# Four small moves at the seams of a two-layer hybrid encoder: a modulation sum's bank, two splits, the last unit's weave, the decays' sums

## The chip, the cores and the metric

The kernel runs on one core of one Trainium2 chip. The metric is the device time of that core in microseconds (us), taken as the median of several runs. Engines are named as in the profile: PE multiplies matrices and writes to banks of the accumulation memory, PEld is its load of weights, DVE, ACT and POOL work element by element, and SP issues transfers (DMA). Each engine takes its own instructions in the order in which they were written, and waits on semaphores of the others.

## The reference, cut to what matters

The program is one forward pass of two layers on a sequence of 1024 tokens with 1024 channels. Layer 0 is an attention layer, layer 1 a state-space layer (SSD, run in both directions).

```
cond = silu(c)
for i in range(2):
    mod = cond @ mod_w[i] + mod_b[i]            # 3072 numbers: shift, scale, gate
    shift, scale, gate = split(mod, 3)
    hn = rms_norm(x, norm_w[i]) * (1 + scale) + shift
    if i == 0:  y = dilated_attention(hn)       # q, k, v, z = split(hn @ w_in); ... (o * silu(z)) @ w_out
    else:       y = bi_ssd(hn)                  # projections, convolution, decays from dt, scan; ... @ w_out
    x = x + gate * y
return rms_norm(x, final_norm_w)
```

In layer 0 there are 24 heads in three patterns of dilation, and the three outputs of a head position are weighted by a softmax over the patterns (`alpha`). In layer 1 `dt = softplus(dt_raw + bias)`, and the decays are exponentials of cumulative sums of `-dt * a` inside chunks of 128 tokens.

## The kernel before, in words

Activations lie channels by tokens, in tiles of 128 channels by 1024 tokens. A float32 product is made of three matmuls: each operand is split into a rounded high part (a cast on ACT, line 271) and the rest (a subtraction on DVE, line 272), and high by high, high by low and low by high are summed in one bank (`mm3`, lines 376 to 378; `out_items`, lines 1000 to 1002). So before a product can start, its weights and its input must have been split. The 27 tiles of the pool `big` hold inputs in split form, outputs of units and weights of the modulation.

The engines' instructions stand in the order in which Python calls them. A block of work is a list of items with a cost and a function, and `weave(main, side)` calls the side's items between the main's, spread in proportion to the costs.

**Layer 0** has twelve units, a unit being two heads of one pattern. For each unit `attn_dense` makes four blocks of products (q, k, v, z), each of 8 steps of 6 matmuls, and into these 32 steps the attention of the unit before is woven (`attn_items`): high and low parts of q and k (`high` on ACT, `low` on DVE, lines 648 to 657), `vprep` (transposes of v, line 633), and for eight blocks of tokens `A` (scores: four matmuls into a bank of the tag `a0`, of which there are two; masked maximum on DVE, line 690; exponential on ACT, line 695), `B` (transposes of the weights, line 704, into the one bank of the tag `a2`; copied out by DVE, line 706) and `C` (product with v, line 719, bank `a3`; multiplied on DVE into the unit's `act` tile, line 730). `stats` sends the maxima and sums out through `a2` (line 743). `vprep` writes to `a2` too.

The modulation of the later uses is computed during layer 0: for each block of 128 outputs DVE multiplies and adds (lines 182 to 188), and after every fourth block `mod_sum` sums over partitions on PE (line 212, four sums, each printed by the profile as two matmuls) into the bank `a2`, from which DVE reads (line 214, and line 217 for scales). There are eight such sums, between 151 and 513 us.

**The last unit has no next unit.** Its attention (11 in count from 0) is woven into `out0`, the output projection: `out_passes` makes four passes (two halves of the tokens, two halves of the outputs) of 12 steps, each of 12 matmuls. In the first pass the steps use the `act` tiles of the units 0 to 11 in order. `prep(r, k)` splits `act[k]` for the half r, and `get` splits up to three steps ahead; the tiles 9 to 11 are ready only after the last mixing over the patterns (`mix_items(3)`: statistics loaded, exponentials, ratios, a broadcast through memory, three products on DVE at line 804). So `first` runs nine steps of the first pass with the last attention in between, nine steps of the second pass with the mixing in between, and then the rest of both.

**Layer 1** begins with three blocks whose steps run alone, then group 0 of eight. Into the steps of group 0 `dt_items` is woven, which computes `dt` and the decays: `tok` and a series on DVE, `end` (`da`, line 1263), `rows` (cumulative sums of `da` on PE, line 1273, total at line 1281, copied by ACT and sent to memory), `back` (transposes of the sums, line 1295, then DVE). Empty items (`wait`) with a cost set the places. DVE also takes the convolution's taps there (line 1330).

Of the kernel before, what the change touches and what calls it, by code (L numbers as in the profile page):

```python
# [12 lines left out]
F32R = mybir.dt.float32r  # L13
# [4 lines left out]
P = 128  # L18
# [3 lines left out]
H2 = 512  # L22
# [33 lines left out]
def weave(main, side):  # L56

    tm = sum(it[0] for it in main) or 1
    tsd = sum(it[0] for it in side) or 1
    i = a = 0  # L60
    b = 0.0
    for c, f, *_ in main:
        f()
        a += c
        while i < len(side) and (b + side[i][0] / 2) / tsd <= a / tm:
            side[i][1]()
            b += side[i][0]
            i += 1
    while i < len(side):
        side[i][1]()  # L70
        i += 1
# [20 lines left out]
class Trunk:  # L92
# [114 lines left out]
    def mod_sum(self, i, b, accs):  # L207

        nc = self.nc
        p = self.bank("a2", [P, 4, P])  # L210
        for k in range(4):
            nc.tensor.matmul(p[:, k, :1], accs[:, k], self.ones[:, :1], start=True, stop=True)
        m = self.modv[i]
        nc.vector.tensor_add(m[:, b:b + 4], p[:, :, 0], self.vec[:, 16 + 24 * i + b:20 + 24 * i + b])
        if b < 16:
            d = b // 2
            nc.vector.scalar_tensor_tensor(self.gs[i][:, d:d + 2], m[:, b + 1:b + 4:2], 1.0,
                                           self.vec[:, 64 + 8 * i + d:66 + 8 * i + d], op0=OP.add, op1=OP.mult)
# [594 lines left out]
    def layer0(self):  # L813
# [80 lines left out]
        r, v = [[self.u(t, [P, H2], F32, n) for _ in range(2)] for t, n in (("pt", 4), ("sm", SM))]  # L894
        u = self.big()
# [60 lines left out]
        side = []  # L956
        mods = self.mod_items(0, list(range(16, 24))) + self.mod_items(1, list(range(24)))
        for u in range(12):
            weave(self.attn_dense(u), side)
            side = self.attn_items(u)  # L960
            k = -(-len(mods) // (7 - u)) if u < 7 else 0
            for i in range(k):
                side.insert(len(side) * (i + 1) // (k + 1), mods.pop(0))
            if UNITS[u][1] == 0 and u:
                m = self.mix_items(UNITS[u][0] - 1)
                n = len(side)
                for i, (at, f) in enumerate(m):
                    side.insert(round(at * n) + i, (1, f))
# [152 lines left out]
    def norm_items(self, st, t, n, item):  # L1121
# [10 lines left out]

        return [(1, total), (1, start), (1, end)] + [(1, lambda kt=kt: item(kt, st["r", t])) for kt in range(KT)]

    def out0(self, tail):


        nc, io = self.nc, self.io
        self.x1d = self.scratch("x1d", [KT, P, S])
        self.hn = hn = [[None] * KT for _ in range(2)]  # L1140
        xin, x1, cut, st = {}, {}, {}, [{} for _ in range(2)]

        def prep(r, k):
            if (r, k) not in cut:
                h = cut[r, k] = self.big(F32R)
                self.split(h[:, :H2], h[:, H2:], self.act[k][:, H2 * r:H2 * r + H2])

        def get(r):
            def f(kt):
                new = (r, kt) not in cut  # L1150
                for k in range(kt, min(kt + 3, 12)):
                    if r or k < 9 or kt >= 9:
                        prep(r, k)
                if new:
                    self.flush()
                return cut[r, kt]
            return f

        def ahead(kt):
            if 8 <= kt < 11:  # L1160
                prep(1, kt - 8)

        def load(r, m):
            xin[m] = self.u("xin", [P, H2], F32, 5)
            nc.sync.dma_start(xin[m], io["xT"][m][:, H2 * r:H2 * r + H2])

        def evac(r, m, t, n, a):
            if t == 0:
                x1[r, m] = self.u("x1", [P, H2], F32, 9)
            x = x1[r, m][:, t:t + n]  # L1170
            nc.vector.scalar_tensor_tensor(x, a, self.gate(0, m), xin[m][:, t:t + n], op0=OP.mult, op1=OP.add)
            nc.gpsimd.dma_start(self.x1d[m][:, H2 * r + t:H2 * r + t + n], x)
            self.sum_squares(st[r], m, x, t, n)

        def after(r, t, n):
            return self.norm_items(st[r], t, n, lambda kt, rstd: self.hn_tile(
                1, kt, H2 * r + t, n, x1[r, kt][:, t:t + n], rstd, hn))

        def first(ps):
            weave(ps[0][:9], tail[1][:1] + tail[0])  # L1180
            weave(ps[1][:9], tail[1][1:])
            self.phase("w1")
            nc.scalar.preload_act_table_set(LN_EXP)
            return [p[9:] for p in ps]

        return self.out_passes("wout0", 12, 4, get, ahead, load, evac, after, first)


# [28 lines left out]
    def dt_items(self):  # L1217
# [73 lines left out]
        def back():  # L1291
            self.lo_engine = nc.vector
            p = self.bank("a0", [P, C, 64], 2)
            for c in range(C):
# [9 lines left out]
        wait = (lambda: None)  # L1304
        return ([(200, wait), (100, tok), (100, ratio), (500, wait)]
                + [(80, lambda k=k: series(k)) for k in range(15, 1, -2)]
                + [(100, end), (300, wait), (100, rows), (200, wait), (100, back), (700, wait)])

    def group_dense(self, g):

# [380 lines left out]

    def main(self):
        self.setup()
        side = self.layer0()
        side = self.out0(side)
        side = self.layer1(side)
        self.out1(side)
        self.phase(None)
# [92 lines left out]
```

## Time and profile before

| what | value |
|---|---|
| runs | 1871.14 us median of 3 (1870.12 to 1874.98) |
| the profiled execution: own time | 1870.17 us |
| its span | 1868.0 us |
| PE busy | 1781.9 us (95%) |
| PEld busy | 1457.3 us (78%) |
| DVE busy | 1421.3 us (76%) |
| ACT busy | 956.5 us (51%) |
| POOL busy | 327.2 us (18%) |
| mean granted clock of PE | 0.982 of full |

A row of a timeline gives the start and the duration in us, the engine, the line, the operation with the tiles written and read, and in brackets the idle time of the engine just before and what ended it. A row of a table by stretches gives the stretch, its length, the busy time of each engine with the number of its instructions, the granted clock of PE, the busy share of the DMA engines and GB/s. Times are counted from the start of the span.

### The profile page before, as it was taken

Reading aid. Unit: us, or ns where it says so; the run is one execution under the profiler, and the core shown is the slowest. Engines: PE = TensorE matmul, PEld = TensorE weight load, DVE = VectorE, ACT = ScalarE, POOL = GpSimd, SP = SyncE. Lnnn points to the kernel's source line nnn. Section 1 sums busy time; section 2 is a strip of 40 time slices with the busy share of each in tenths; the row PEclk is TensorE's granted clock in tenths of the full one; section 3 lists DMA queues with packets and bytes.
Section 4 is the critical chain, followed back from the end, with each engine's and each line's share of the span. In section 5 each row is a group of like instructions: output and inputs, shape, how many; then the busy total and the mean of one; then the engine's idle time right before and its main releaser. Section 6 shows DMA issues by size and latency. Waiting matters only on the chain.

```text
span 1868.0 us, 28492 instructions
## 1 busy us (share of the span) xinstructions
PE 1781.9 (95%) x10050; PEld 1457.3 (78%) x10050; DVE 1421.3 (76%) x3219; ACT 956.5 (51%) x2095; POOL 327.2 (18%) x493
## 2 busy tenths in 40 slices
PE   5899999999999999999999999999999999789997
PEld 3678788778788888778978788888888878567787
DVE  7866578666755555666686989898998989897975
ACT  5454445444545544544435656565656565565632
POOL 4611112112211221010110101010101010224310
PEclk7899999999999999999999999999999999999998
DMA  6242234223411221264213233424334243344543
GB/s 252 92 124 89 84 107 132 66 89 91 125 47 55 58 77 52 68 213 139 96 51 84 75 111 75 117 82 115 89 93 105 76 111 82 113 123 143 187 158 101
DMA packets 99734, 193.66 MB, mean 104 GB/s; under 512 B 15624, under 2 KB 23048, under 8 KB 99592
## 3 DMA queue, kind: packets, MB, share of 16 engines
q1 hardware_dynamic: 86600, 167.32, 29.6%
q0 software_dynamic: 12288, 23.86, 4.7%
q8 instruction: 80, 1.31, 0.3%
q10 hardware_dynamic: 704, 0.66, 0.1%
q14 instruction: 62, 0.51, 0.1%
HBM read 169.00 MB, written 16.48 MB: 99 GB/s over the span
## 4 chain that ended last, share of the span: by engine, by line
PE 39%; DVE 11%; ACT 3%; DMA 2%; issue 2%; SPq 0%; POOL 0%; DVEq 0%; ACTq 0%; POOLq 0%
PE acc L376 8%; PE acc L378 7%; PE acc L377 7%; PE a L1481 3%; PE a L1419 2%; DVE big L1330 2%; PE a L1000 2%; PE a L1001 2%; PE a L1002 2%; DVE wlo L272 2%; PE acc L1002 1%; PE acc L1000 1%; PE acc L1001 1%; DVE W L1465 1%; DVE acs L1470 1%
## 5 line engine op out<-in xcount | busy, mean ns | idle before, releaser
L376 PE MATMUL acc<-big,whi 128*128 128x512 f32 (+1 forms) x1520 | 631.5, 415 | 12.6 <-ACT big L293 11.9
L377 PE MATMUL acc<-big,whi 128*128 128x512 f32 (+1 forms) x1520 | 595.7, 392 | 2.7 <-DVE big L294 2.6
L378 PE MATMUL acc<-big,wlo 128*128 128x512 f32 (+1 forms) x1520 | 596.4, 392 | 0.3 <-DVE wlo L272 0.3
L376 PEld LDWEIGHTS acc<-big,whi 128*128 128x128 f32 x1520 | 288.3, 190 | 78.3 <-issue 15.7
L378 PEld LDWEIGHTS acc<-big,wlo 128*128 128x128 f32 x1520 | 287.7, 189 | 64.4 <-DVE wlo L272 1.2
L377 PEld LDWEIGHTS acc<-big,whi 128*128 128x128 f32 x1520 | 288.9, 190 | 52.8 <-DVE big L294 5.9
L272 DVE TENSOR_TENSOR wlo<-wraw,whi 128x512 fp32r<-128x512 f32 (+1 forms) x297 | 215.4, 730 | 83.4 <-ACT whi L271 80.4
L271 ACT CAST whi<-wraw 128x512 fp32r<-128x512 f32 (+1 forms) x302 | 181.5, 612 | 82.8 <-PE a L1001 30.0
L695 ACT ACTIVATE sm<-sm,nb 128x256 f32<-128x256 f32 (+1 forms) x192 | 89.3, 466 | 198.8 <-DVE nb L693 196.1
L1330 DVE SCALAR_TENSOR_TENSOR big<-acc,cv,big 128x512 f32<-128x512 f32 (+1 forms) x248 | 169.4, 743 | 6.5 <-ACT big L1322 6.5
L1489 POOL TENSOR_TENSOR big<-big,yt 128x128 f32<-128x128 f32 x128 | 65.3, 530 | 588.2 <-DVE yt L1485 588.1
L1451 ACT ACTIVATE E<-E,nacb 128x128 f32<-128x128 f32 x256 | 81.9, 391 | 144.1 <-DVE E L1443 130.3
L706 DVE COPY pt<-a 128x512 f32<-128x512 f32 (+1 forms) x96 | 57.6, 600 | 76.6 <-PE a L704 76.5
L690 DVE CUSTOM_DVE_ANT_0 sm<-a,cst 128x256 f32<-128x256 f32 (+1 forms) x192 | 65.0, 376 | 65.1 <-PE a L685 64.8
L1000 PE MATMUL a<-big,whi 128*128 128x256 f32 (+1 forms) x304 | 99.3, 327 | 0.0
L1002 PE MATMUL a<-big,wlo 128*128 128x256 f32 (+1 forms) x304 | 98.2, 323 | 0.5 <-DVE wlo L272 0.5
L1001 PE MATMUL a<-big,whi 128*128 128x256 f32 (+1 forms) x304 | 97.9, 322 | 0.0
L1001 PE MATMUL acc<-big,whi 128*128 128x512 f32 x224 | 88.8, 396 | 6.1 <-DVE big L1556 4.3
L592 POOL DMA_DIRECT2D rt<-kT x92 | 50.3, 559 | 251.0 <-ACT kT L532 150.6
L1002 PE MATMUL acc<-big,wlo 128*128 128x512 f32 x224 | 89.3, 399 | 3.3 <-DVE wlo L272 2.7
L1000 PE MATMUL acc<-big,whi 128*128 128x512 f32 x224 | 90.5, 404 | 1.3 <-ACT big L271 1.2
L1322 ACT ACTIVATE big<-acc,cv 128x512 f32<-128x512 f32 x62 | 44.5, 769 | 86.4 <-PE acc L378 76.1
(254 smaller groups left out, 3186.6 us busy)
## 6 DMA issues: line engine op xcount, KB each, us to landing
wraw<-in_win SPq DMA_DIRECT2D x186, 256.0 KB
acs<-acsd SPq DMA_DIRECT2D x64, 512.0 KB
wraw<-in_wout SPq DMA_DIRECT2D x112, 256.0 KB
big<-in_modw SPq DMA_DIRECT2D x48, 512.0 KB
yd<-big POOLq DMA_DIRECT2D x14, 512.0 KB, 4.5
big<-yd SPq DMA_DIRECT2D x28, 256.0 KB
vT<-mix POOLq DMA_DIRECT2D x20, 256.0 KB, 4.7
big<-in_xT SPq DMA_DIRECT2D x8, 512.0 KB
```

Of the source, the lines that this page charges most:

```text
L271: self.nc.scalar.copy(dst_hi, src)
L272: self.late.append((lambda: self.lo_engine.tensor_sub(dst_lo, src, dst_hi.bitcast(F32)), tile))
L376: mm(o, hi[:, cols], x_[:, t0:t0 + n], start=first, stop=False, **kw)
L377: mm(o, hi[:, cols], x_[:, H2 + t0:H2 + t0 + n], start=False, stop=False, **kw)
L378: mm(o, lo[:, cols], x_[:, t0:t0 + n], start=False, stop=last, **kw)
L695: nc.scalar.activation(sm[:, h, :W], sm[:, h, :W], AF.Exp, bias=nb[:, h:h + 1], scale=0.125, accum_out=stat[:, h, 1, i:i + 1])
L1000: mm(o, hi[:, c], x[:, t:t + n], start=kt == 0 and (n == H2 or m % 2 == 0), stop=False, **kw)
L1001: mm(o, hi[:, c], x[:, H2 + t:H2 + t + n], start=False, stop=False, **kw)
L1002: mm(o, lo[:, c], x[:, t:t + n], start=False, stop=kt == nkt - 1, **kw)
L1330: nc.vector.scalar_tensor_tensor(y[:, lo:hi], a[:, lo + o:hi + o], w[:, cv, k:k + 1], y[:, lo:hi], op0=OP.mult, op1=OP.add)
L1451: nc.scalar.activation(E[:, h], E[:, h], AF.Exp, bias=self.nacb[:, c, 4 * g + h:4 * g + h + 1])
L1489: nc.gpsimd.tensor_mul(z, z, t[:, r])
```

## The change

It has four parts, and no operation is added or taken out.

1. `mod_sum` takes a bank of the tag `a0` (two, shared with the scores) in place of the one bank `a2`.
2. The splits of `act[0]` and `act[1]` for the first half of the tokens, made so far at the first step of the output projection, are called before the last of the 32 steps of unit 11. `prep` becomes the method `act_split` and its table the attribute `cut0`.
3. The last unit's attention is woven into 8 steps of the first pass instead of 9, and the mixing into the ninth step and the nine of the second pass.
4. In `dt_items` the empty item before `rows` costs 450 for 300, the one between `rows` and `back` 100 for 200, and the one after it 650 for 700: the sum stays 1200.

```diff
@@ def mod_sum(self, i, b, accs):
-        p = self.bank("a2", [P, 4, P])
+        p = self.bank("a0", [P, 4, P], 2)
@@ def layer0(self):
         for u in range(12):
-            weave(self.attn_dense(u), side)
+            d = self.attn_dense(u)
+            if u == 11:
+                for k in range(2):
+                    d.insert(len(d) - 1, (1, lambda k=k: self.act_split(0, k)))
+            weave(d, side)
@@
+    def act_split(self, r, k):
+
+        if (r, k) not in self.cut0:
+            h = self.cut0[r, k] = self.big(F32R)
+            self.split(h[:, :H2], h[:, H2:], self.act[k][:, H2 * r:H2 * r + H2])
+
     def out0(self, tail):
...
-        xin, x1, cut, st = {}, {}, {}, [{} for _ in range(2)]
-
-        def prep(r, k):
-            if (r, k) not in cut:
-                h = cut[r, k] = self.big(F32R)
-                self.split(h[:, :H2], h[:, H2:], self.act[k][:, H2 * r:H2 * r + H2])
+        xin, x1, cut, st = {}, {}, self.cut0, [{} for _ in range(2)]
+        prep = self.act_split
...
         def first(ps):
-            weave(ps[0][:9], tail[1][:1] + tail[0])
-            weave(ps[1][:9], tail[1][1:])
+            weave(ps[0][:8], tail[1][:1] + tail[0])
+            weave(ps[0][8:9] + ps[1][:9], tail[1][1:])
@@ def dt_items(self):
-                + [(100, end), (300, wait), (100, rows), (200, wait), (100, back), (700, wait)])
+                + [(100, end), (450, wait), (100, rows), (100, wait), (100, back), (650, wait)])
@@ def main(self):
         self.setup()
+        self.cut0 = {}
```

Three places show what this does to the order. The first is PE in unit 5's time, at the modulation sum that stands before unit 4's first transposes of v (L212 the sum into a bank, L633 the transposes into the bank `a2`; in brackets the semaphores waited for). Before:

```order
L378 MATMUL acc_3178<-big_612,wlo_3122 128x512
L212 MATMUL a_576_3276<-ones_67,big_2699 128x1 [waits DMAHW2_49,Activation_49]
L212 MATMUL a_576_3276<-ones_67,big_2699 128x1 x2
L212 MATMUL a_576_3276<-ones_67,big_2699 128x1 [waits DVE_49]
L633 MATMUL a_577_3283<-cst_71,vT_3010 128x128 [waits DVE_49]
L633 MATMUL a_577_3283<-cst_71,vT_3010 128x128 x3
```

Now:

```order
L378 MATMUL acc_3178<-big_612,wlo_3122 128x512
L212 MATMUL a_576_3276<-ones_67,big_2699 128x1 [waits DMAHW2_49]
L212 MATMUL a_576_3276<-ones_67,big_2699 128x1 x2
L212 MATMUL a_576_3276<-ones_67,big_2699 128x1 [waits DVE_49]
L633 MATMUL a_577_3283<-cst_71,vT_3010 128x128 [waits Activation_49]
L633 MATMUL a_577_3283<-cst_71,vT_3010 128x128 x3
```

No row moves; the transposes wait for ACT's copy out of `a2` instead of DVE's read of the sum.

The second is DVE from the end of unit 11's dense blocks into the output projection (L272 is the low part of a split: of an `act` tile where it writes `big`, of a weight where it writes `wlo`; L654 to L657 are the low parts of q and k, eight operations a half). Before, first the stretch with the first half of q and k, then the next rows:

```order
L272 TENSOR_TENSOR big_7062<-big_806,big_7062 128x512 [waits Activation_49]
L272 TENSOR_TENSOR big_7064<-big_1388,big_7064 128x512 [waits Activation_49]
L272 TENSOR_TENSOR big_7066<-big_1972,big_7066 128x512 [waits Activation_49]
L654 TENSOR_TENSOR Q_1252_7051<-kT_6631,Q_1252_7051 64x512 [waits DMASW5_49,DMASW1_49,Activation_49]
...
L272 TENSOR_TENSOR wlo_7075<-wraw_6874,whi_7074 128x512 [waits DMAHW3_49]
L272 TENSOR_TENSOR big_7107<-big_2524,big_7107 128x512 [waits Activation_49]
L272 TENSOR_TENSOR wlo_7113<-wraw_6952,whi_7112 128x512 [waits DMAHW4_49,PE_49,Activation_49]
L654 TENSOR_TENSOR Q_1252_7051<-kT_6631,Q_1252_7051 64x512 [waits Activation_49]
```

Now:

```order
L272 TENSOR_TENSOR big_7036<-big_806,big_7036 128x512 [waits Activation_49]
L272 TENSOR_TENSOR big_7038<-big_1388,big_7038 128x512 [waits Activation_49]
L654 TENSOR_TENSOR Q_1254_7057<-kT_6631,Q_1254_7057 64x512 [waits DMASW5_49,DMASW1_49,Activation_49]
...
L272 TENSOR_TENSOR big_7068<-big_1972,big_7068 128x512
L272 TENSOR_TENSOR wlo_7074<-wraw_6874,whi_7073 128x512 [waits DMAHW3_49]
L654 TENSOR_TENSOR Q_1254_7057<-kT_6631,Q_1254_7057 64x512 [waits Activation_49]
...
L272 TENSOR_TENSOR big_7107<-big_2524,big_7107 128x512
L272 TENSOR_TENSOR wlo_7113<-wraw_6952,whi_7112 128x512 [waits DMAHW4_49,PE_49,Activation_49]
```

The low part of `act[2]` now stands behind the first half of q and k, and that of `act[3]` with its weights behind the second half.

The third is PE in group 0 of layer 1, around `rows` (L1273 before, L1279 now; L1281 and L1287 its total). Before:

```order
L378 MATMUL acc_9146<-big_8716,wlo_9079 128x512
L1273 MATMUL a_1662_9184<-cst_71,big_9012 32x128 [waits DVE_49,PE_49]
L1273 MATMUL a_1662_9184<-cst_71,big_9012 32x128 x7
L1273 MATMUL a_1663_9194<-cst_71,big_9012 32x128 [waits PE_49]
L1273 MATMUL a_1663_9194<-cst_71,big_9012 32x128 x7
L1281 MATMUL a_1664_9205<-big_9012,ones_67 128x512 [waits Activation_49]
L376 MATMUL acc_9145<-big_8092,whi_9113 128x512
```

Now:

```order
L378 MATMUL acc_9146<-big_8716,wlo_9079 128x512
L376 MATMUL acc_9145<-big_8092,whi_9113 128x512 [waits Activation_49]
L377 MATMUL acc_9145<-big_8092,whi_9113 128x512
L378 MATMUL acc_9145<-big_8092,wlo_9114 128x512 [waits Pool_49]
L376 MATMUL acc_9146<-big_8721,whi_9113 128x512
L377 MATMUL acc_9146<-big_8721,whi_9113 128x512
L378 MATMUL acc_9146<-big_8721,wlo_9114 128x512
L1279 MATMUL a_1662_9192<-cst_71,big_9012 32x128 [waits DVE_49,PE_49]
L1279 MATMUL a_1662_9192<-cst_71,big_9012 32x128 x7
```

One step of six matmuls has moved ahead of `rows`; `back` stays where it was among the steps.

## Rows read from the trace of the kernel before

**Rows 1.** The page, part 1: busy time, share of the span, instructions.

```profile
PE 1781.9 (95%) x10050; PEld 1457.3 (78%) x10050; DVE 1421.3 (76%) x3219; ACT 956.5 (51%) x2095; POOL 327.2 (18%) x493
```

**Rows 2.** PE's waits, whole span: for whom; us in total, times, longest.

```profile
PE a L633 <- DVE modv L214: 4.0, 2, 3.7
...
PE a L704 <- DVE modv L214: 0.3, 1, 0.3
```

**Rows 3.** Timeline, 344 to 356 us: the fifth modulation sum.

```profile
349.51 0.69 DVE L654 TENSOR_TENSOR Q<-kT,Q 64x512 fp32r<-64x512 f32 x1
350.14 0.95 PE L212 MATMUL a<-ones,big 128*128 128x1 f32 x8
...
353.94 0.69 DVE L272 TENSOR_TENSOR wlo<-wraw,whi 128x512 fp32r<-128x512 f32 x1
354.54 0.15 DVE L214 TENSOR_TENSOR modv<-a,vec 128x4 f32<-128x4 f32 x1
...
354.76 1.11 PE L633 MATMUL a<-cst,vT 128*128 128x128 f32 x4 [3.67 <-DVE modv L214]
```

**Rows 4.** Busy time by stretches: us, PE, PEld, DVE, ACT, POOL, clock, DMA, GB/s.

```profile
124.00:128.00 4.00, 4.00 (x15) 3.28 (x14) 3.14 (x13) 2.22 (x9) 0.00 (x0) 0.59 0.68 227
...
354.76:360.00 5.24, 5.24 (x17) 4.46 (x18) 0.81 (x4) 3.82 (x4) 0.00 (x0) 0.50 0.46 150
...
967.20:971.80 4.60, 4.60 (x35) 3.48 (x36) 4.60 (x8) 1.16 (x2) 0.59 (x1) 0.63 0.02 4
...
1060.00:1085.00 25.00, 22.41 (x152) 17.71 (x151) 21.19 (x48) 19.35 (x39) 4.72 (x10) 1.00 0.28 94
```

**Rows 5.** Busy time by stretches, one stretch of dense steps alone.

```profile
940.00:950.00 10.00, 10.00 (x45) 8.26 (x45) 9.23 (x12) 3.66 (x7) 1.95 (x2) 1.00 0.12 32
```

**Rows 6.** Timeline, PE and DVE: the longest wait of scores, and the fourth sum.

```profile
123.43 0.39 PE L684 MATMUL a<-K,Q 128*128 128x256 f32 x1 [2.09 <-DVE stat L690]
...
297.95 0.08 DVE L690 DVE_READ_ACCUMULATOR2_ANT stat<- 128x1 f32 x1
298.06 0.94 PE L212 MATMUL a<-ones,big 128*128 128x1 f32 x8
```

**Rows 7.** Timeline, 748 to 765 us: from the last dense block into the output projection.

```profile
748.12 1.29 ACT L549 ACTIVATE big<-acc 128x512 f32<-128x512 f32 x2 [7.99 <-PE acc L378]
...
749.45 1.65 ACT L271 CAST big<-big 128x512 fp32r<-128x512 f32 x3
...
750.12 0.50 PE L1000 MATMUL acc<-big,whi 128*128 128x512 f32 x1 [1.23 <-ACT big L271]
...
757.20 0.69 DVE L272 TENSOR_TENSOR wlo<-wraw,whi 128x512 fp32r<-128x512 f32 x1
...
757.95 0.50 PE L1002 MATMUL acc<-big,wlo 128*128 128x512 f32 x1 [0.68 <-DVE wlo L272]
...
764.83 0.28 PE L685 MATMUL a<-L,Q 128*128 128x256 f32 x1
```

**Rows 8.** Timeline, PE, 783 to 816 us: last attention, statistics, ninth unit's tile.

```profile
783.57 0.41 PE L704 MATMUL a<-cst,sm 128*128 128x128 f32 x2 [1.31 <-DVE pt L706]
...
788.58 0.28 PE L743 MATMUL a<-cst,stat 128*32 128x128 f32 x1
...
815.07 0.50 PE L1001 MATMUL acc<-big,whi 128*128 128x512 f32 x1 [1.49 <-DVE big L272]
```

**Rows 9.** Timeline, 966 to 990 us: the decays' sums in layer 1.

```profile
967.20 3.10 PE L1273 MATMUL a<-cst,big 128*32 128x128 f32 x32 [3.10 <-DVE big L1263]
...
975.88 0.71 PE L1295 MATMUL a<-cst,big 64*128 64x64 f32 x8
...
984.40 1.07 ACT L1334 ACTIVATE big<-big 128x1024 f32<-128x1024 f32 x1
...
987.54 0.81 PE L1406 MATMUL a<-cst,big 128*128 128x128 f32 x6
```

**Rows 10.** Timeline, PE, layer 1's scan: a wait under 2 us.

```profile
1067.28 0.66 PE L1481 MATMUL a<-acs,SS 128*64 128x128 f32 x8 [1.94 <-DVE acs L1470]
```

## The prediction

> **What bounds the kernel now.** I read the page's table of engines first, then PE's waits, then the timeline at each of the four seams that the change touches, and last the table by stretches for the clock. PE is busy for 1781.9 of 1868.0 us [rows 1], so the kernel is faster only where PE stands still or runs at the half clock. Its waits at these seams are few and short. A modulation sum holds the transposes behind it three times: 3.67 us once, 0.33 once, and 0.3 before a transpose of weights [rows 2, 3]. At the first step of the output projection it waits 1.23 us for a split, and 0.68 at the third [rows 7]. The last attention has one wait of 1.31 between two neighbouring transposes, and the tile that needs the last mixing is 1.49 late [rows 8]. The decays' sums wait 3.10 [rows 9].
>
> The clock comes on top. Where PE stood 3.67 us, the next 5.24 us ran at a granted clock of 0.50, which is 1.2 GHz of the two levels [rows 3, 4]; after 3.10 us the next 4.60 ran at 0.63 in the mean [rows 4, 9]; after a wait of 2.09 four us ran at 0.59 [rows 4, 6]. After one of 1.94 the clock stayed at 1.00 [rows 4, 10].
>
> One dense matmul costs 10.00 us by 45, 0.222 us [rows 5]. So a step of layer 0 or 1 (6 matmuls) costs 1.33 us, one of the projection (12) 2.67 us.
>
> **Part 1, the sum's bank.** At 350 us the transposes (L633) wanted the one bank in which the sum lay, and DVE read that sum only after the eight operations of a half of q and k, from 349.51 to 353.94, and a weight's low part [rows 3]. With the sum in a scores' bank the order shows L633 waiting for ACT alone, whose copy was made long before. PE then goes on at 351.1: transposes, one step, the first scores in the other bank, two steps, and only then the scores that need the sum's bank, at about 351.1 + 0.6 + 1.33 + 0.5 + 2.67 = 356.2, when the sum has been read for 1.5 us (354.7). So the 3.67 goes whole, and with it the half clock: 5.24 x (1 - 0.50) = 2.6 us. With the two small waits, 3.67 + 2.6 + 0.33 + 0.3 = **6.9 us**. What hides the sum's wait now is those steps; without them it would come back at the scores. Five of the eight sums stand among scores and take one of their two banks. The nearest case is the fourth, where the maximum that frees the bank ended at 297.95 and the sum began at 298.06 [rows 6]; there and at the other four I count nothing. Lower end 0.6 (the large wait returns at the next instruction), upper end 6.9, since nothing more waits there. I take the upper end, because the semaphores of the changed order name no late event.
>
> **Parts 2 and 3, the seam into the projection and the last attention.** The two casts move into 7.99 us in which ACT idles [rows 7], and cost nothing; without that cover they would hold back the SiLU of the last block by 2 x 0.55. The first step can start at 748.9 instead of 750.12. But DVE is late next. ACT has 1.65 / 3 x 2 = 1.1 us less to do before q and k, so DVE's row of low parts also comes 1.1 earlier, at the third step's weights 757.20 - 1.1 = 756.1. The low part of `act[2]` now stands there first (0.61, as they follow each other), then the weights' (0.69): 757.4, against 757.95 before [rows 7]. Of the 1.23 us only 0.5 is left. PE reaches the third step at 748.9 + 2 x 2.67 + 0.6 = 754.8 and stands some 1.8 us for the one (756.7) and 0.6 for the other.
>
> At the fourth step it turns. Its low parts stood before the second half of q and k; now they stand behind its eight operations: 757.4 + 4.4 (the same eight operations took 349.51 to 353.94, rows 3) = 761.8, + 0.61 + 0.69 = 763.1. The rest of the step and the third scores take 9 x 0.222 + 0.5 = 2.5: 765.6, where the same work ended at 764.83 + 0.12 before [rows 7]. That is a loss of 0.7, counted from before.
>
> Later it gains twice. The neighbouring transposes that waited 1.31 get a step of the projection between them. And the statistics leave one step, 2.67 us, earlier in PE's work, while the chain from them (loads, exponentials, ratios, broadcast) is timed by ACT, DVE and transfers; so the 1.49 at the late tile is covered, with 1.2 to spare [rows 8]. SP gets the broadcast one weight load earlier, and the loads behind it wait with it; four weight buffers are ahead, as before. Sum: -0.7 + 1.31 + 1.49 = **2.1 us**. Lower end: the clock falls once in the two new waits (1.7, the value at the decays below) and the 1.31 stays: -0.7 - 1.7 + 1.49 = -0.9. Upper end: the fourth step's wait does not come, 0.5 + 1.31 + 1.49 = 3.3.
>
> Whether those waits cost clock is open by the rows: 1.94 did not lower it, 2.09 did, and the longer piece is 1.8. I take no fall. The Trainium skill, "TensorE: Matmul & The Clock Gate", Part 1, says that the gate's measuring is free-running and does not start with the kernel's own events, so that one gap may lower the clock in one position and not in another; by that rule 1.7 us of this term would hang on the phase. No run shown here tells it.
>
> **Part 4, the decays' sums.** `da` is ready by DVE at 967.1, whatever PE does. One step, 1.33 us, now runs before the sums, so the wait shrinks from 3.10 to 1.8, and the step is done in it. A wait of 1.8 is nearer to 1.94, which left the clock alone, than to 2.09; so I also count 4.60 x (1 - 0.63) = 1.7. Sum **3.0 us**. Behind it, PE comes to the transposes of group 0 (L1406) at 987.54 - 3.0 = 984.5, and the last SiLU for them ended at 984.40 + 1.07 = 985.5 [rows 9], but `back` and DVE's work behind it come earlier too. Lower end 0.6 (the clock falls all the same and 0.7 is given back), upper end 3.0.
>
> **Sum.** 6.9 + 2.1 + 3.0 = 12.0 us off the profiled execution's 1870.17: 1858.2. That execution stood 0.97 below the median of the runs, so the forecast for a median is **1859.1 us**. By the ends alone it would be 6.9 + 2.1 + 3.0 down to 0.6 - 0.9 + 0.6 = 0.3 us.
>
> **The rivals.** (a) DVE sets the pace at both seams. It is busy for 4.60 of 4.60 us around the decays [rows 4], which speaks for it. Then the projection's part is -0.9 and the decays' 1.3, with the 6.9 kept: 7.3 us, 1863.8. (b) The sum's large wait returns behind another DVE result at 354 us, since DVE was busy for nearly the whole of it; then part 1 gives 0.6, and with 2.1 + 3.0 the time is 1865.4. Against it speak the semaphores and DVE's idling after 354.7: 0.81 of the next 5.24 us busy [rows 4]. (c) The scores pay: at the five sums among scores the bank of two blocks ago is not yet free, PE waits there as long as the longest wait of scores on record, 2.09, and loses 1.7 of clock each time: 5 x 3.8 = 19 us lost against 12.0 won, 7.0 on the median of 1871.14: 1878.1, slower than before. It decides as soon as a sum arrives over 2 us before the maximum two blocks back is done; the fourth sum arrived 0.1 after it [rows 6], which speaks against it, as do four steps or more between scores elsewhere. (d) The early splits do not do what they should: they wait for PE to release a tile, and if that is the tile of the step just before, ACT holds the SiLU behind them, and the first step starts as late as before; the 0.5 is lost and 0.5 more: 1860.1.
>
> **How the numbers follow.** Forecast 0.55, (a) 0.22, (b) 0.13, (c) 0.05, (d) 0.05. A difference of 0.3%, 5.6 us, is about what a measurement of this kernel can tell from no change, so "faster" means under 1865.5. The forecast, (d), most of (a) (0.17) and half of (b) (0.06) lie there: 0.83; (c) is slower: 0.05; the rest, 0.12, is no change. The range is 1855.0 to 1867.5: above it takes in (a) and (b) with 2 us for the spread of runs (1870.12 to 1874.98), below the upper end of the projection's part (1.2 more), and one fall of the clock somewhere later (1.7 each) that a shifted phase may spare.
>
> **What the changed profile would show.** Part 1: no wait of the transposes of v for the modulation, clock 1.00 in the stretch after the fifth sum, and no new wait of scores there. Parts 2 and 3: the first projection step directly behind the statistics, a wait of about 2 us for DVE at the third step and another at the fourth, none between the last transposes, none at the late tile. Part 4: a wait of about 1.8 us before the sums and a clock of 1.00 behind it. The prediction is wrong if scores wait for the modulation, if the two DVE waits together exceed what the late tile gives back, or if the saved time reappears as a wait of the first transposes of group 0.

## The result, and the profile after

The changed kernel takes 1858.09 us (median of 4 runs, 1856.54 to 1858.78), the kernel before beside it 1870.9 (4 runs, 1870.12 to 1874.98): a ratio of 0.993, 95% interval 0.9915 to 0.9944. That is 12.8 us less; 12.0 were forecast. The profiled execution took 1857.47 us, its span is 1855.5.

The page's table of engines, after [rows 1 before]:

```profile
span 1855.5 us, 28487 instructions
PE 1777.3 (96%) x10050; PEld 1453.4 (78%) x10050; DVE 1420.6 (77%) x3219; ACT 956.6 (52%) x2095; POOL 328.0 (18%) x493
```

The work is the same. PE's busy time is 4.6 us lower, which fits with fewer products at the half clock or behind a wait; no run separates the two over the whole span.

PE's waits, after (for whom; us in total, times, longest):

```profile
PE acc L1005 <- DVE big L272: 2.7, 2, 1.7
...
PE a L684 <- DVE stat L690: 2.4, 1, 2.4
...
PE a L1279 <- DVE big L1269: 1.8, 1, 1.8
...
PE a L704 <- DVE pt L706: 1.3, 2, 0.7
```

No line waits for the sums' reader (L214) any more [rows 2], and the scores (L684) have only the one wait of before at 124 us. The 2.7 are the two new waits of the projection. The waits of L704 for DVE that are left are of at most 0.7. Beyond line 955 the change shifts the numbers: L1000 to L1002 are now L1004 to L1006, L1273 is L1279, L1406 is L1412.

The fifth sum in the timeline, after [rows 3], and the stretches behind it and behind the decays' sums [rows 4]:

```profile
350.51 0.95 PE L212 MATMUL a<-ones,big 128*128 128x1 f32 x8
...
351.32 0.64 PE L633 MATMUL a<-cst,vT 128*128 128x128 f32 x4
...
353.18 0.28 PE L684 MATMUL a<-K,Q 128*128 128x256 f32 x1
...
354.93 0.15 DVE L214 TENSOR_TENSOR modv<-a,vec 128x4 f32<-128x4 f32 x1
...
356.40 0.28 PE L684 MATMUL a<-K,Q 128*128 128x256 f32 x1
```

```profile
354.00:360.00 6.00, 6.00 (x32) 5.09 (x31) 5.47 (x24) 4.67 (x12) 2.20 (x4) 1.00 0.53 165
958.19:962.80 4.61, 4.61 (x42) 3.62 (x43) 4.61 (x8) 2.70 (x10) 0.73 (x1) 1.00 0.14 28
```

DVE still reads the sum late, 3.5 us behind its end (354.93, the sum ends at 350.51 + 0.95), but PE is at dense steps and comes to the scores that share the bank at 356.40. The clock is 1.00 in both stretches, where it was 0.50 and 0.63.

The seam into the projection in the timeline, after [rows 7, 8]:

```profile
741.71 1.29 ACT L549 ACTIVATE big<-acc 128x512 f32<-128x512 f32 x2 [6.94 <-PE acc L378]
...
742.20 0.27 PE L743 MATMUL a<-cst,stat 128*32 128x128 f32 x1
742.23 0.48 PE L1004 MATMUL acc<-big,whi 128*128 128x512 f32 x1
...
749.74 0.69 DVE L272 TENSOR_TENSOR big<-big,big 128x512 fp32r<-128x512 f32 x1
750.48 0.50 PE L1005 MATMUL acc<-big,whi 128*128 128x512 f32 x1 [1.74 <-DVE big L272]
...
755.48 0.69 DVE L272 TENSOR_TENSOR big<-big,big 128x512 fp32r<-128x512 f32 x1
756.22 0.50 PE L1005 MATMUL acc<-big,whi 128*128 128x512 f32 x1 [0.95 <-DVE big L272]
...
759.58 0.29 PE L685 MATMUL a<-L,Q 128*128 128x256 f32 x1
...
777.33 0.41 PE L704 MATMUL a<-cst,sm 128*128 128x128 f32 x2
...
778.63 0.28 PE L743 MATMUL a<-cst,stat 128*32 128x128 f32 x1
...
802.12 1.22 DVE L804 TENSOR_TENSOR big<-big,kT 128x1024 f32<-128x1024 f32 x1
...
805.98 0.39 PE L1004 MATMUL acc<-big,whi 128*128 128x512 f32 x1
```

The first step (742.23) stands directly behind the statistics and waits for nothing, the third waits 1.74 and the fourth 0.95 for a low part on DVE; the wait of 1.31 between the last transposes and the one of 1.49 at the late tile are gone. The decays' sums, after [rows 9]:

```profile
958.19 1.94 PE L1279 MATMUL a<-cst,big 128*32 128x128 f32 x32 [1.78 <-DVE big L1269]
...
973.62 1.07 ACT L1340 ACTIVATE big<-big 128x1024 f32<-128x1024 f32 x1
975.54 0.82 PE L1412 MATMUL a<-cst,big 128*128 128x128 f32 x6
```

The wait is 1.78, and the first transposes of group 0 start 0.85 us after the last SiLU before them (973.62 + 1.07 = 974.69).

**Where the time went.** To split the difference, I count the dense products of lines 376 and 1000 (1004) and compare the start of the n-th one in two profiles. The first column is its start in the kernel before; the others say how much earlier (-) or later it starts in another profile.

| product | before | changed | bank alone | splits alone | 8 steps alone | rows alone | four splits |
|---|---|---|---|---|---|---|---|
| 101st | 138.65 | +1.07 | -0.17 | -0.45 | -0.20 | -1.14 | -1.13 |
| 521st (behind the sums) | 528.27 | -6.41 | -7.65 | -0.71 | -0.52 | -1.92 | -8.59 |
| 766th (before the seam) | 745.31 | -6.41 | -7.65 | -0.71 | -0.52 | -1.92 | -8.58 |
| 851st (behind the late tile) | 821.77 | -8.99 | -3.69 | +2.85 | -2.04 | +0.15 | -12.19 |
| 1101st (before the decays) | 949.38 | -9.00 | -3.70 | +2.87 | -1.84 | +0.25 | -12.19 |
| 1181st (group 0) | 1022.81 | -11.95 | -3.86 | +2.78 | -3.47 | -2.72 | -15.20 |
| 1801st | 1619.65 | -12.14 | -4.01 | +3.01 | -3.61 | -2.89 | -15.38 |
| last | 1854.75 | -12.95 | -1.94 | +6.74 | -3.05 | -2.77 | -14.35 |

In the changed kernel the modulation sums gave 7.5 us (from +1.07 to -6.41), the seam 2.6 (to -8.99), the decays' sums 3.0 (to -11.95). The rest, +1.07 in the first 139 us and -0.8 behind 1620 us, lies where no instruction was moved; there the profiles differ by up to 3.7 us with the same code (the last two rows of "bank alone" and "splits alone").

The column "before" is one execution, and at the fifth sum it was a slow one. From the 326th to the 346th product all ten profiles with the new bank save the same 6.32 us, but the three others with the old bank are themselves 0.43, 0.43 and 0.92 us quicker there than this one, with the same wait of 3.7. So the 7.5 us of the sums would be 6.7 to 7.2 against those.

### The profile page after: what moved, and what is told of

It is laid out like the page before. It is cut to its first block, busy times and chain, and to the rows that moved or that the text cites. A ratio compares the mean times of both kernels' runs of the same rounds, so it can differ in the third digit from the quotient of the medians.

```text
span 1855.5 us, 28487 instructions
## 1 busy us (share of the span) xinstructions
PE 1777.3 (96%) x10050; PEld 1453.4 (78%) x10050; DVE 1420.6 (77%) x3219; ACT 956.6 (52%) x2095; POOL 328.0 (18%) x493
## 4 chain that ended last, share of the span: by engine, by line
PE 72%; DVE 17%; ACT 4%; issue 3%; DMA 3%; SPq 0%; ACTq 0%; DVEq 0%; POOL 0%
PE acc L376 16%; PE acc L378 15%; PE acc L377 15%; PE a L1487 3%; PE a L1425 2%; DVE wlo L272 2%; PE a L719 2%; PE a L1004 2%; PE a L1005 2%; PE a L1006 2%; DVE big L1336 2%; PE a L704 2%; PE acc L1006 2%; PE acc L1004 2%; PE acc L1005 2%
## 5 line engine op out<-in xcount | busy, mean ns | idle before, releaser
L272 DVE TENSOR_TENSOR wlo<-wraw,whi 128x512 fp32r<-128x512 f32 (+1 forms) x297 | 214.1, 726 | 83.1 <-ACT whi L271 80.1
L1004 PE MATMUL a<-big,whi 128*128 128x256 f32 (+1 forms) x304 | 99.2, 326 | 0.0
L1006 PE MATMUL a<-big,wlo 128*128 128x256 f32 (+1 forms) x304 | 98.2, 323 | 0.1
L1006 PE MATMUL acc<-big,wlo 128*128 128x512 f32 x224 | 89.5, 399 | 3.2 <-DVE wlo L272 2.4
L1004 PE MATMUL acc<-big,whi 128*128 128x512 f32 x224 | 90.5, 404 | 0.0
```

What stands on the lines that cost most here:

```text
L272: self.late.append((lambda: self.lo_engine.tensor_sub(dst_lo, src, dst_hi.bitcast(F32)), tile))
L1004: mm(o, hi[:, c], x[:, t:t + n], start=kt == 0 and (n == H2 or m % 2 == 0), stop=False, **kw)
L1006: mm(o, lo[:, c], x[:, t:t + n], start=False, stop=kt == nkt - 1, **kw)
```

## The experiments

**Each part alone, on the kernel before.** Four kernels, run on one chip; the kernel before beside them took 1875.29 us (17 runs, 1871.24 to 1880.59).

Part 1, the bank:

```diff
-        p = self.bank("a2", [P, 4, P])
+        p = self.bank("a0", [P, 4, P], 2)
```

> The kernel before with the sum's bank alone changed (part 1). Theory: the transposes' wait for the fifth sum (3.67 us) goes with the half clock behind it (2.6 us), and some 0.6 us of small waits: 6 to 7.5 us less than before, about 1864; no wait for the modulation on record, granted clock 1.00 for the 5 us behind the fifth sum, and the waits at 750, 815 and 967 us of before stand as they were, only earlier. Rival: the scores share the bank, so a scores' wait of 1 us or more appears next to one of the eight sums and eats part of it: under 4 us gained. Second rival: the clock fell for another reason than the 3.67 us, and a half-clock stretch of 5 us is still there near 350 us: about 4 us gained.

Measured: ratio 0.9944 (0.9922 to 0.9965). By the table the sums give 7.5 us (-0.17 to -7.65), as in the changed kernel, and no wait for L214 is left; both rivals fall. Behind that stands something that was not expected: the late tile is 4.04 us late.

```profile
780.87 0.28 PE L743 MATMUL a<-cst,stat 128*32 128x128 f32 x1
...
806.84 1.23 DVE L804 TENSOR_TENSOR big<-big,kT 128x1024 f32<-128x1024 f32 x1 [1.72 <-DMA kT<-mix]
...
809.93 0.79 PE L1001 MATMUL acc<-big,whi 128*128 128x512 f32 x1 [4.04 <-DVE big L272]
```

Part 2, the early splits (the change's `act_split` and the loop in `layer0`, all else as before):

```diff
+            if u == 11:
+                for k in range(2):
+                    d.insert(len(d) - 1, (1, lambda k=k: self.act_split(0, k)))
```

> The kernel before with the two early splits alone (part 2; attention still in 9 steps). Theory: the first step starts 1.23 us earlier, the third then waits about 1.8 us for the low part of the third tile, which DVE makes behind eight operations for q and k; the fourth step waits for nothing, since its low parts still stand before the second half of q and k; the waits of 1.31 and 1.49 stay. Net 0.3 to 0.9 us less than before. Rival: the early splits are what makes the fourth step wait in the changed kernel (0.95 us there); then that wait shows here too and the net is between no gain and 0.7 us lost.

Measured: ratio 0.9990 (0.9979 to 1.0). PE, in its timeline:

```profile
756.18 0.50 PE L1005 MATMUL acc<-big,whi 128*128 128x512 f32 x1 [1.72 <-DVE big L272]
```

That is the only wait over 0.2 us in the first four steps, and from the seam to behind the third scores the kernel gains 0.48 us (-0.71 to -1.19 at the 794th product). The fourth step doesn't wait, so the rival falls. Then the late tile takes 3.98 us, and the clock falls behind it.

Part 3, the last attention in 8 steps:

```diff
-            weave(ps[0][:9], tail[1][:1] + tail[0])
-            weave(ps[1][:9], tail[1][1:])
+            weave(ps[0][:8], tail[1][:1] + tail[0])
+            weave(ps[0][8:9] + ps[1][:9], tail[1][1:])
```

> The kernel before with the last attention in 8 steps alone (part 3; no early splits). Theory: the first step's 1.23 and the third's 0.68 stay, the fourth step waits 1.0 to 1.5 us newly, since its low parts now stand behind the second half of q and k; the waits of 1.31 between the last transposes and 1.49 at the late tile go, with about 0.9 us of slow starts and short gaps around them: 1.8 to 2.6 us less than before. Rival: the late tile is early in the changed kernel because of the early splits, not of the 8 steps; then a wait of 1 to 1.5 us stays at the tenth step and the net is under 1 us.

Measured: ratio 0.9960 (0.9945 to 0.9975); the seam gives 1.5 us (-0.52 to -2.04), 0.3 under what was expected.

```profile
749.60 0.49 PE L1000 MATMUL acc<-big,whi 128*128 128x512 f32 x1 [1.23 <-ACT big L271]
...
757.44 0.50 PE L1002 MATMUL acc<-big,wlo 128*128 128x512 f32 x1 [0.65 <-DVE wlo L272]
...
763.21 0.50 PE L1001 MATMUL acc<-big,whi 128*128 128x512 f32 x1 [1.58 <-DVE big L272]
```

The new wait stands at the fourth step, and there is none at the late tile: both belong to the 8 steps, as the theory had it. A second thing was not expected. The decays' sums wait 3.12 us here, much as in the kernel before, and the clock does not fall; without the half clock the place takes 1.6 us less (-1.84 to -3.47), though nothing was moved there:

```profile
965.36:969.96 4.60, 4.60 (x42) 3.64 (x43) 4.60 (x8) 2.70 (x10) 0.73 (x1) 1.00 0.13 28
```

Part 4, the decays' sums:

```diff
-                + [(100, end), (300, wait), (100, rows), (200, wait), (100, back), (700, wait)])
+                + [(100, end), (450, wait), (100, rows), (100, wait), (100, back), (650, wait)])
```

> The kernel before with the decays' sums one step later alone (part 4). Theory: the wait shrinks from 3.10 to about 1.8 us, and a wait of that length leaves the clock at 1.00: 3.0 us less than before. Rival: whether the clock falls hangs on where the gap lies in time and not on its length; here the gap lies some 9 us later than in the changed kernel, and a half-clock stretch may follow it: 1.3 us less.

Measured: ratio 0.9970 (0.9955 to 0.9984); the place gives 3.0 us (+0.25 to -2.72), with a wait of 1.78 and a clock of 1.00 behind it. The late tile's wait of only 1.91 us lowered the clock in this profile (first row):

```profile
813.59:819.00 5.41, 5.41 (x17) 4.28 (x18) 3.65 (x6) 1.14 (x2) 0.00 (x0) 0.68 0.49 145
967.44:972.00 4.56, 4.56 (x42) 3.58 (x43) 4.56 (x8) 2.65 (x9) 0.73 (x1) 1.00 0.11 23
```

**The late tile.** In these profiles the last product of the mixing (L804 with kT) starts 23.40 us behind the statistics (L743) in the kernel before, 23.84 in "rows alone", 25.93 and 25.97 in "splits alone" and "bank alone", with the same code between them; what differs is when the transfers land. The repeat of the bank alone was to tell whether the bank does it:

> The kernel before with the sum's bank alone, repeated. Its first profile showed the late tile 4.04 us late where the kernel before had 1.49. Theory that the chain of transfers behind the statistics varies from one execution to another (the last product came 25.97 us behind the statistics there, 23.40 in the kernel before): the wait lies anywhere from 1.4 to 4.1 us and goes with that distance less 21.9 us. Rival, that the changed bank itself delays the late tile: again about 4 us at the same distance. At the wait of some 2.2 us at 124 us, where the clock fell in four of ten profiles, no forecast; behind the sums' 3.1 us it fell in four of five, and should fall again.

Measured in one run: 1868.62 us. The product came 24.35 us behind the statistics and the wait was 2.42; by the rule in the expectation 24.35 - 21.9 = 2.45. So the bank does not do it, the chain's length does. The chain's 2.6 us of spread are spread in the wait one to one, as long as attention takes 9 steps. With 8 steps PE reaches that tile 27.34 to 27.36 us behind the statistics instead of 24.62 to 24.64 and it didn't wait over 0.2 us there in any of the nine profiles with 8 steps; but in those the chain took 23.1 to 24.1 us, so how a chain of 25.9 fares there was not seen. The changed kernel was run again beside three variants:

> The changed kernel once more, beside the three that follow. By the profiles so far 11 to 14 us less than before. The theory of the late tile (its chain of transfers takes 0 to 2.5 us longer from one execution to another, and the 8 steps give 2.5 us of room) expects no wait at the tenth step, or one under 0.5 us, also where the kernels of the last runs waited 4 us; the rival, that the 4-us waits come from the parts that these kernels lack, expects that as well, so only a wait of over 1 us here speaks against both.

Measured: 1860.05 us against 1874.51 (7 runs), ratio 0.9926 (0.9911 to 0.9941); no wait at the tenth step, with a chain of 23.81. At the three places 7.4, 2.6 and 3.0 us.

**Part 4 undone in the changed kernel** (the diff above backwards):

> The changed kernel with part 4 undone: the decays' sums come one step sooner again and PE waits 3.1 us. Theory that the length of the gap sets the clock: a half-clock stretch follows, 3.0 us more than the changed kernel. Rival, that the gap's place in time decides as well (one kernel had a 3.12-us gap there and kept its clock): the clock stays at 1.00 in about one execution in four, and then it is 1.3 us more.

Measured: 1862.0 us, ratio 0.9936 (0.9915 to 0.9956). The wait is back, the clock falls, and 3.0 us are missing at that place (the products there are 11.1 us ahead before it and 11.2 behind it, where the changed kernel goes from 9.0 to 12.0). The whole time is 1.95 us above the changed kernel's 1860.05, but the runs of the two overlap, so the 3.0 rests on the place. The wait and the stretch behind it:

```profile
956.09 3.47 PE L1279 MATMUL a<-cst,big 128*32 128x128 f32 x32 [3.12 <-DVE big L1269]
```

```profile
956.09:960.70 4.61, 4.61 (x36) 3.87 (x37) 4.61 (x8) 1.21 (x3) 0.23 (x1) 0.66 0.02 4
```

**Four early splits.**

```diff
-                for k in range(2):
+                for k in range(4):
```

> The changed kernel with the splits of four tiles instead of two made early. Theory that DVE's order sets the two new waits: the third step waits only for its weights' low part, 1.2 us instead of 1.85 in two pieces and 0.6 sooner; at the fourth the wait stays near 0.9 us, for the weights' low part, and its end comes 1.5 to 2 us sooner; 1.5 to 2 us less than the changed kernel at the end of the projection's first steps, and the rest unchanged. Rival: ACT or a tile that is not yet released holds the two further splits, so the last block's SiLU comes later: no gain, up to 1 us more.

> The changed kernel with four early splits, once more beside the two POOL kernels. By its first profile: waits of 1.1 and 0.9 us at the third and fourth step, and 1 us less than the changed kernel between the last layer-0 block and the tenth step; against the kernel before 0.7 to 1.0%. If the 1 us was luck of one execution, the same stretch is as long as in the changed kernel here.

Measured: 1856.72 us, ratio 0.9912 (0.9895 to 0.9928), beside the changed kernel's 1860.05; in a second set of runs 1857.08, ratio 0.9914 (0.9896 to 0.9931). PE at the third and the fourth step:

```profile
747.89 0.50 PE L1006 MATMUL acc<-big,wlo 128*128 128x512 f32 x1 [1.13 <-DVE wlo L272]
...
753.20 0.50 PE L1006 MATMUL acc<-big,wlo 128*128 128x512 f32 x1 [0.90 <-DVE wlo L272]
```

Both waits are now for the weights' low part, as DVE's order had it. The seam gives 3.6 us (-8.58 to -12.19) and 3.9 in the repeat, against 2.6 twice in the changed kernel and 2.4 with part 4 undone, which has the same seam: 1.0 to 1.6 us better, at or under the lower end of the 1.5 to 2 expected. The intervals of the whole times overlap, so the times alone don't show it.

**Low parts on POOL.** With four early splits, `on_pool` sets the engine of the low parts to POOL while the second and the third step are issued, so the weights' low parts for the third and fourth step are made there; in the first of the two kernels the decays' sums also come one more step later.

```diff
+            for k in (1, 2):
+                ps[0][k] = (ps[0][k][0], lambda f=ps[0][k][1]: on_pool(f))
...
-                + [(100, end), (450, wait), (100, rows), (100, wait), (100, back), (650, wait)])
+                + [(100, end), (600, wait), (100, rows), (100, wait), (100, back), (500, wait)])
```

> The changed kernel with four early splits, the weights' low parts of the third and fourth step on POOL instead of DVE, and the decays' sums one more step later. Theory: nothing at the third and fourth step stands behind DVE's eight operations any more, both waits shrink to under 0.5 us and 3 to 3.6 us go; the sums' wait of 1.8 shrinks to about 0.4 and 1.3 us go: 4 to 5 us less than the changed kernel. Rival: the scores need the same eight operations, so PE stands at them instead, under 2 us gained at the seam; or the transposes of group 0 wait for ACT and give back the 1.3.

Measured: 1859.28 us, ratio 0.9923 (0.9908 to 0.9937), no better than the changed kernel. Both halves of the rival came true. In its timeline:

```profile
745.94 3.11 DVE L656 CAST K<-K 64x512 fp32r<-64x512 f32 x1
746.22 2.54 POOL L272 TENSOR_TENSOR wlo<-wraw,whi 128x512 fp32r<-128x512 f32 x2
...
756.72 0.36 PE L684 MATMUL a<-K,Q 128*128 128x256 f32 x1 [1.47 <-DVE stat L690]
...
972.94 0.33 PE L1419 MATMUL a<-cst,big 128*128 128x128 f32 x1 [0.49 <-ACT big L1347]
973.88 0.66 PE L1419 MATMUL a<-cst,big 128*128 128x128 f32 x4 [0.62 <-ACT big L1347]
```

The third and fourth steps wait for nothing, but the next scores wait 1.47 for DVE; the seam gives 4.3 us (-6.69 to -11.0). The sums wait for nothing, and the first transposes of group 0 wait for ACT's SiLU instead: that place gives 1.5 us (-11.0 to -12.5) where the changed kernel has 3.0. The 4 to 5 us expected beyond the changed kernel came to 0.8. With the sums put back:

> The changed kernel with four early splits and the weights' low parts of the third and fourth step on POOL, the decays' sums where the changed kernel has them. Theory: the loss of the last kernel lay in the sums that came one step too early for ACT's SiLU; so the first transposes of group 0 wait for nothing here, the sums wait 1.8 us again, and 1.5 us of that kernel's 2.8 lost come back. At the seam no wait at the third and fourth step, about 1.5 us at the scores, and 0.5 to 0.8 us less than with four splits alone. Rival: the loss came from POOL's work; then the transposes still wait.

Measured: 1857.2 us, ratio 0.9914 (0.9893 to 0.9934). The transposes wait for nothing, the sums 1.73 us, that place gives 3.0 and the seam 4.3: the loss lay in the sums' place. Against four splits beside it (1857.08) nothing is gained that a time can show.

One cast on DVE (L656), 0.42 us beside an idle POOL, took 3.11 while POOL worked. With one subtraction on POOL instead of two (`for k in (1,):`):

> As before, but only the third step's low part on POOL. In the kernel with two such subtractions on POOL (2.54 us) one cast of k on DVE (line 656) took 3.11 us in place of 0.42. Theory that the cast and POOL shut each other out: with one subtraction the cast takes 1.6 to 2.0 us and ends 0.2 to 0.4 us behind POOL. Rival, that the cast waited for something else: 0.42 or about 3.1 us.

Measured in one run: 1858.08 us.

```profile
743.24 1.07 POOL L762 DMA_DIRECT2D mf<-stat  x2 [0.44 <-DMA stat<-sm]
...
744.05 1.87 DVE L656 CAST K<-K 64x512 fp32r<-64x512 f32 x1
...
744.33 1.30 POOL L272 TENSOR_TENSOR wlo<-wraw,whi 128x512 fp32r<-128x512 f32 x1
...
753.70 0.79 PE L1006 MATMUL acc<-big,wlo 128*128 128x512 f32 x1 [2.78 <-DVE wlo L272]
```

The cast ends at 745.92, 0.29 us behind POOL's 745.63, and in the kernel with two at 749.05, 0.29 behind 748.76. So POOL's subtraction shuts the cast out for its whole length. The first row shows that POOL was already at work when the cast began: it issued transfers until 744.31 and went straight on to the subtraction. With four early splits and no subtraction on POOL, the same cast began during the same row and took 0.50, ending 0.25 us behind it:

```profile
743.23 1.07 POOL L762 DMA_DIRECT2D mf<-stat  x2 [0.44 <-DMA stat<-sm]
...
744.05 0.50 DVE L656 CAST K<-K 64x512 fp32r<-64x512 f32 x1
```

With one subtraction on POOL the fourth step waits 2.78 us for the other, made on DVE (last row of the first of these two blocks), the clock falls behind it (0.64 in the next 4.5 us), and the seam gives only 2.0 us.

## Why the prediction was right, point by point

**Part 1, forecast 6.9, measured 7.5.** The mechanism is the one forecast, shown by the bank alone. The fifth sum gave 6.3 us (the products on its two sides, the 326th and the 346th, start 0.38 later and 5.95 earlier), forecast 3.67 + 2.6 = 6.27. The small waits were put at 0.33 + 0.3; the products around three other sums move by 0.49, 0.22 and 0.54, 1.2 together (between the 151st, 231st and 291st, and between the 401st and 461st). The idle time there was 0.35, 0.11 and 0.33 in the profile of before: a third wait, before a transpose of weights at 301 us, was missed. The term also counted idle time alone, and a product behind a wait takes longer itself, 0.50 instead of 0.39 us [rows 7]. That the large wait came within 0.05 us of its forecast is luck of one execution: the forecast was made from the profile that is the slowest of four there, and against the others the new bank gives 5.4 to 5.9. Rivals (b) and (c) fall: no scores wait for the modulation, in any of the ten profiles with the new bank.

**Parts 2 and 3, forecast 2.1, measured 2.6.** Rival (d) falls: the first step starts directly behind the statistics (742.23). The third step's wait was forecast at 1.8 and is 1.74; the 0.5 gained there was 0.48 in the splits alone. The fourth step's loss was put at 0.7; the third scores stand at 759.58 where the shift of 6.41 before the seam would have put them at 758.42, so it is 1.16. DVE's low part came when worked out (755.48; 761.8 - 6.41 = 755.39), but from the product that needs the weights' low part (756.83) the rest of the step and the scores took 2.87 us where 2.5 had been counted. Behind it 2.80 was forecast and 3.7 came (from behind the third scores to the second group of products of the late step, 765.00 to 815.64 us before and 759.70 to 806.66 after: 50.64 us against 46.96). 2.9 of it were idle gaps in PE's timeline, and by the stretches PE's busy time fell from 47.42 to 46.66, which fits the slow starts behind waits again. Two errors of 0.5 and 0.9 us, of opposite sign, so part of the agreement is luck. By its letter one of the prediction's signs of being wrong came: the two waits for DVE, 1.74 and 0.95, exceed the 1.49 of the late tile. That sign was badly drawn, since the first of them stands in the place of the 1.23 and 0.68 of before; counted as in the sum, 1.16 was lost and 3.7 won.

The term 1.49 was the shortest of the late tile's waits: 1.49, 1.91, 2.42, 3.98 and 4.04 us in the five profiles with 9 steps. So in another execution part 3 is worth more than forecast: up to 2.7 us of wait in place of 1.49 (PE comes 2.72 us later with 8 steps), and the clock behind it. The prediction took one execution's transfers for a constant.

**Part 4, forecast 3.0, measured 3.0**, and the 1.78 us before the sums are the 1.8 of the forecast. The wait of group 0's transposes that the prediction named as its danger did not come, with 0.85 us to spare; one step later it came, and cost 2.8 us (from 15.36 to 12.54 us ahead between the 1141st and the 1181st product). But of the 3.0 us, 1.7 are the clock, and the reason given for them was wrong. The prediction read a border out of two rows (1.94 keeps the clock, 2.09 lowers it). The 14 profiles of this study show none. The table counts, at places that recur, in how many the clock fell from 1.00 behind the wait (a mean between 0.50 and 1.00 is a stretch partly at the half clock):

| place | length of the wait, us | profiles in which the clock fell behind it |
|---|---|---|
| fifth sum, old bank | 3.67 to 3.69 | 4 of 4 |
| decays' sums, old place | 3.10 to 3.15 | 5 of 6 (not behind 3.12 in one) |
| late tile, 9 steps | 1.49 to 4.04 | 3 of 5 (4.04, 3.98 and 1.91; not 2.42 and 1.49) |
| scores at 124 us | 1.95 to 2.51 | 6 of 14 (2.51 both ways) |
| scan at 1052 to 1070 us | 1.90 to 1.95 | 1 of 14 |
| scan at 1585 to 1603 us | 2.66 to 2.69 | 5 of 14 |
| scan's state products (line 1419 before), 1612 to 1632 us, mostly with a shorter wait 1.4 us later | 2.91 to 3.76, once 2.15 | 14 of 14 |
| decays' sums, new place | 1.73 to 1.78 | 0 of 7 |

The Trainium skill, "TensorE: Matmul & The Clock Gate", Part 1, cited in the prediction, has the measuring free-running; the prediction drew from it that the same gap may lower the clock in one position and not in another. The runs agree with that: 2.51 us at 124 us left the clock at 1.00 in the splits alone and brought it to 0.68 in the first POOL kernel. What decides between the two they don't show. Taken without their places, of all PE's waits over 1.4 us between 77 and 1640 us in the 14 profiles (before 77 us they stand in groups), the clock fell behind none of 30 under 1.85 us, 2 of 17 up to 2.0, 7 of 16 up to 2.6, 6 of 15 up to 2.85 and 24 of 25 longer ones. So in this kernel a wait has a chance of costing clock that in the main grows with its length, and the 1.7 us of part 4 and the 2.6 of part 1 are to be counted with theirs: 5 of 6 and 4 of 4 here. A single wait's length is not all of it: in the kernel before the clock also fell at 73.5 us, behind waits of 0.28 and 0.88 (0.51 from 73.5 to 77.0). The two stretches at 124 us, splits alone and first POOL kernel:

```profile
124.60:129.00 4.40, 4.40 (x25) 3.85 (x26) 3.54 (x15) 2.60 (x9) 0.00 (x0) 1.00 0.74 220
```

```profile
124.44:129.00 4.56, 4.56 (x18) 3.91 (x19) 3.71 (x16) 2.60 (x9) 0.00 (x0) 0.68 0.70 234
```

**The sum.** 7.5 + 2.6 + 3.0 = 13.1 us by the three places, against 12.0. The median fell by 12.8, and by 14.5 beside the second set of the changed kernel. The kernel before took 1870.12 to 1880.59 us in its runs here, so that the forecast lies within a microsecond of the first measurement is partly luck; the three places carry the argument. Rival (a), DVE setting the pace at both seams, is half true: DVE's order does set both new waits, as the four splits and the POOL kernels show, but at the size that the forecast had already counted.

## What to carry to other kernels

A wait that an in-order engine's reader causes (a sum read 3.5 us late) can be removed by giving the result a bank that the next instructions don't need (hurrying the reader instead was not tried here); look for the next user of that bank, and count the work in between. Price a wait with the slow start behind it and with a chance that the clock falls, and take the late arrival of a chain of transfers from several executions. Before moving work one step later, look at who stands ready behind it: here the first step was worth 3.0 us and the second took back 1.5.

## What was not expected of the hardware

- The same chain (loads, exponentials, broadcast through memory) took 23.1 to 26.0 us from the statistics to the last product, in 14 profiles.
- A cast on DVE stood for the whole of POOL's subtraction, over two in a row (3.11 us for 0.42). The Trainium skill, "SBUF — State Buffer", section "SBUF: two separate sides", says that GpSimd and some operations of DVE (those in a two-port mode or with two inputs in SBUF) share a pair of ports under an exclusive lock, that the one that starts first holds it for its whole instruction, and that the other blocks. The trace agrees on the blocking. On the order it doesn't speak against the page: the cast's row begins 0.28 us before the subtraction's, but inside POOL's transfer issues before it, and no run here has the cast begin while POOL is idle just ahead of a subtraction.
- Waits of 1.91 and 1.94 us can lower the clock, and one of 3.12 can leave it alone: in the kernel with one low part on POOL the scan's wait of 1.94 brought it to 0.60, at the place where the prediction had read that such a wait leaves the clock alone [rows 10].

```profile
1053.20:1057.50 4.30, 3.82 (x27) 3.33 (x28) 4.20 (x14) 3.23 (x11) 0.92 (x2) 0.60 0.16 61
```
